# Squared relu on ACT, twelve couples first, finer operand work, and block 2's first half of tokens completed ahead of the second

## The chip, the core and the metric

The kernel runs on one NeuronCore of a Trainium2 chip. The core has five engines with an instruction queue each: PE (TensorE, matrix products into the accumulation memory PSUM), DVE (VectorE), ACT (ScalarE), POOL (GpSimd) and SP (SyncE, which here only issues transfers). They run side by side and wait for each other through semaphores. The metric is device time in microseconds (us), the median of several runs. Before the change it is 2611.3 us (three runs, 2607.07 to 2614.02).

## The reference

The program is two transformer blocks in a row over 1024 tokens of width 1024, all in fp32. Both end in the same kind of MLP. Cut to what matters here:

```python
# block 1: attention over a window of 128 tokens + gated delta rule, then
h = h + jnp.concatenate([attn_out, dn_out], axis=-1) @ w_o
m = rmsnorm(h, norm_mlp)
h = h + jnp.square(jax.nn.relu(m @ w_up)) @ w_down          # w_up 1024x4096, w_down 4096x1024
h = h + sigmoid(rmsnorm(h, norm_ple) @ w_ple_gate) * (p @ w_ple_proj)
x = rmsnorm(h, norm_final)
# block 2: pooled mixer + HGRN2 recurrence in chunks over 6 heads, then
x = x + jnp.concatenate([y_pool, y_hgrn], axis=-1) @ w_out
h2 = rms_norm(x, norm_mlp_g)
x = x + jnp.square(jax.nn.relu(h2 @ w_up)) @ w_down
return rms_norm(x, final_norm_g)
```

## The kernel before

Activations lie transposed, features on the 128 partitions and tokens along the row, in tiles of 128 x 512. So a stream of width 1024 is 8 tiles for each of the two halves of the tokens, h = 0 and h = 1.

**Three products for one.** Each fp32 operand is split into a rounded high part and the rest (`split`, lines 203 and 204: ACT makes the high part by a cast, DVE the rest by a subtraction), and `acc` (lines 223 to 225) sums three matmuls for each pair of 128-blocks. Weights arrive by `load_w` as rows of 1024 (`wr`), and become `wh` and `wl`; there are two buffers for `wr` and three each for `wh` and `wl`.

**The up projection of the MLP** (`mlp`) does without every eighth product: it cuts both factors into 2 x 2 blocks and makes seven products of sums and differences instead of eight. One step n of 16 ("couple") stands for two 128-rows of the hidden layer. Two of its products need only the first half of the tokens: `first` multiplies by b11 and b21, adds both, and gives hidden row 2n of half 0. The others need operands t1, t2, t3, t4 and b22, which are differences between the halves. For the first HP couples `first` runs ahead, before any of the differences is needed; it keeps the product by b11 (tile `r`) in memory (`p1s`). Each hidden tile gets the squared relu in `out` (line 960, one DVE instruction), and SP stores it to `hid`.

**Operands of the MLP** come from `forms`: for a half, `rms` (squares on ACT, line 259, sums on DVE, line 260, a matmul with ones, line 244, the inverse root in small DVE steps, lines 229 to 234), `spread` (lines 270 and 273), the scaling of eight tiles (line 477), and then for half 0 eight splits, for half 1 sixteen differences (line 489) and twenty splits. `forms` is a task that runs beside other work: it stops at each `yield`, and `tick`, called after each product, takes it on by one step. For half 1 it has 15 stops, the first of which is reached when the task is made.

**Ahead of the MLP of block 2** a `weave` of three lanes runs the twelve recurrences (`hgrn`, head j and half h) and lets a second task, `fill`, put its products between their steps, 0.9 of a step for each round. Once the last input projections are made, `fill` is `out_first`: the output projection over six of the eight mixer blocks, 16 tiles of 18 matmuls, stored to `hm`. When all recurrences are over, `out_last` adds the two blocks of the last two heads (6 matmuls a tile, line 408) for half 0, then for half 1, and `forms` is called after each. Block 1 is built the same way.

The lines of Python give the order in which instructions are made; the framework then sets each engine's own order. Each engine works through its order strictly, so what it has to wait for holds up what stands behind.

Of the kernel before, what the change touches and what calls it, by code (L numbers as in the profile page):

```python
# [11 lines left out]
ACTF = mybir.ActivationFunctionType  # L12
ALU = mybir.AluOpType
# [41 lines left out]
FA, POOL_AT = 5, 2  # L55
GATE_HEAD, GATE_TAIL, IN2_HEAD = 4, 4, 6

HP = 10


@with_exitstack
def block_kernel(ctx: ExitStack, tc: tile.TileContext, A):
    nc = tc.nc
    V, SC, G, PE = nc.vector, nc.scalar, nc.gpsimd, nc.tensor
# [247 lines left out]
    def run(*tasks):  # L312
        for t in tasks:
            for _ in t:
                pass
# [70 lines left out]
    def out_first(mix, rows, W, per, src, dst, *halves):  # L386

        n = [0]

        def ev(i, h, ps):  # L390
            n[0] += 1
            f = tt(("sq", "ac")[n[0] % 2])
            nc.sync.dma_start(out=f, in_=src[cs(i), hs(h)])
            V.tensor_tensor(f, ps, f, ALU.add)
            nc.sync.dma_start(out=dst[cs(i), hs(h)], in_=f)

        x = {}
        for h in halves:
            yield from mixed(mix, h, rows)
            x[h] = mix_in(mix, h, rows)  # L400
        yield from proj(x, W, ev, halves, per=per)

    def out_last(mix, rows, W, per, src, h):

        def ev(i, h, ps):
            x = th(h, i)
            nc.sync.dma_start(out=x, in_=src[cs(i), hs(h)])
            V.tensor_tensor(x, ps, x, ALU.add)
            nc.sync.dma_start(out=res[cs(i), hs(h)], in_=x)
            hh[h][i] = x  # L410

        yield from mixed(mix, h, rows)
        yield from proj({h: mix_in(mix, h, rows)}, W, ev, (h,), per=per)
# [46 lines left out]
    def forms(gname, eps):  # L460


        def go(h):
            g = small(gname, 0, KD)
            r = yield from rms(hh[h], eps)

            def pairs(x, new):
                out = []
                for t in x:
                    hi, lo = new(), new()  # L470
                    split(t, hi, lo)
                    out.append((hi, lo))
                return out

            for k in range(KD):
                t = hh[h][k]
                V.scalar_tensor_tensor(t, t, g[:, k:k + 1], r, ALU.mult, ALU.mult)
                if k % 2:
                    yield
            if h == 0:  # L480
                return pairs(hh[0][:4], tu), pairs(hh[0][4:], tu)
            b11, b21, b12, b22 = hh[0][:4], hh[0][4:], hh[1][:4], hh[1][4:]
            out = {}

            for name, x, a, b, new in (("t1", b11, b12, b11, tu), ("t2", b11, b22, b11, tu), ("t3", b12, b22, b12, trr),
                                       ("b22", b22, None, None, trr), ("t4", b21, b11, b21, trr)):
                if a is not None:
                    for i in range(4):
                        V.tensor_tensor(x[i], a[i], b[i], ALU.subtract)
                    yield  # L490
                out[name] = pairs(x, new)
                yield
            return out

        return Parts(go)

    def trr():
        return tr(F32R)

    xs, hm = dram.tile([D, S], F32, name="xs"), dram.tile([D, S], F32, name="hm")  # L500
    res, hid = dram.tile([D, S], F32, name="res"), dram.tile([4 * D, S], F32, name="hid")
    p1s = dram.tile([HP * 128, H], F32, name="p1s")
    hh = [[None] * KD, [None] * KD]


    mix = mix_new("mix1")
# [428 lines left out]
    un = forms("norm_mlp", 1e-6)  # L935
    wa, wb = [[A["w_o"][4 * p + i] for i in range(4)] for p in range(2)]
# [8 lines left out]
    tasks = [lambda lane, n=n: attn_task(lane, n) for n in range(NC)]  # L945
# [7 lines left out]
    def mlp(u, up, dn, between, before=None):  # L953
# [3 lines left out]
        side[0] = 2  # L957

        def out(i, h, c):
            V.scalar_tensor_tensor(c, c, 0.0, c, ALU.max, ALU.mult)  # L960
            nc.sync.dma_start(out=hid[cs(i), hs(h)], in_=c)

        def product(w, i, x):
# [24 lines left out]
        b11, b21 = u[0]  # L988
        for n in range(HP):
            s = tt("r")  # L990
            first(load_w(up[2 * n]), s, tt("f"), n)
            nc.sync.dma_start(out=p1s[cs(n), :], in_=s)
        x = u[1]
        for n in range(16):
# [21 lines left out]
            c = tt("f")  # L1016
# [13 lines left out]
        for h in range(2):  # L1030
            for c4 in range(2):
# [3 lines left out]
                for g in range(8):  # L1035
                    ws = [load_w(dn[4 * g + 2 * c4 + i]) for i in range(2)]
                    x = []
# [9 lines left out]
                for i in range(4):  # L1047
                    m = 4 * c4 + i
                    t = th(h, m)
# [90 lines left out]
    mix = mix_new("mix2")  # L1140
# [156 lines left out]
    t = ins(True, 0, head=IN2_HEAD)  # L1297
# [5 lines left out]
    un = forms("norm_mlp_2", 1e-5)  # L1303
    wa, wb = [A["w_out_2a"][i] for i in range(8)], [A["w_out_2b"][i] for i in range(2)]

    def fills2():
        for j in range(1, 6):
            yield from ins(False, j)
            done.add(j)
        yield from out_first(mix, range(6), wa, 1, xs, hm, 0, 1)  # L1310

    done = {0}

    def task2(lane, j, h):
        while j not in done:
            next(fill, None)
        yield from hgrn(lane, j, h, *i_.pop((j, h)), j >= 4)

    fill = fills2()
    tasks = [lambda lane, j=j, h=h: task2(lane, j, h) for j in range(6) for h in range(2)]  # L1320
    tasks.insert(POOL_AT, lambda lane: pool_mix(lane, *i_.pop("pool")))
    weave(tasks, fill, lambda: R5)

    run(out_last(mix, range(6, 8), wb, 4, hm, 0))
    un()
    run(out_last(mix, range(6, 8), wb, 4, hm, 1))
    un()

# [131 lines left out]
```

## Time and profile before

| | |
|---|---|
| median of three runs | 2611.3 us |
| the profiled execution, its own time | 2615.59 us |
| its span | 2613.2 us, 2.4 us less |
| PE busy | 2503.3 us, 96% of the span |
| weight loads (PEld) | 2010.0 us, 77% |
| DVE, ACT, POOL busy | 1742.7, 987.3, 377.6 us |
| chain that ended last | PE 66%, issue 3%, DVE 3%, POOL 1%, ACT 1% |

The profile's page gives busy time by engine; PE's is modelled, so a busy PE can still run at half its clock. The table of stretches is the better guide: it gives for each stretch how many instructions each engine had in it, and the clock that PE was granted.

### The profile page before, as it was taken

How to read it: one execution, taken by the hardware profiler on the slowest of the kernel's cores; microseconds unless marked ns; L12 is line 12 of the kernel's file. 1: busy time of each engine (PE TensorE's matmuls, PEld its weight loads, DVE VectorE, ACT ScalarE, POOL GpSimd, SP SyncE). 2: the span in 40 equal slices, each digit the busy share in tenths (PEclk: the TensorE clock that was granted, in tenths of full speed). 3: DMA queues.
4: the chain of work that ended last, by engine and by line, in shares of the span. 5: the costliest groups of instructions: out<-in, count | busy, mean ns of one | idle time of the engine just before them, and what ended most of it. 6: DMA issues, size and time to landing. Idle time of an engine off the chain costs nothing.

```text
span 2613.2 us, 41652 instructions
## 1 busy us (share of the span) xinstructions
PE 2503.3 (96%) x16150; PEld 2010.0 (77%) x16150; DVE 1742.7 (67%) x3189; ACT 987.3 (38%) x1632; POOL 377.6 (14%) x430
## 2 busy tenths in 40 slices
PE   6999999998999999999999999999988999999997
PEld 4766777786788888878877878887767888888886
DVE  8787787869887675465457643446599876655653
ACT  4477444324222254344333332333242222444441
POOL 5612222200000000000022343344200000000000
PEclk8999999999999999999999999999989999999998
DMA  5311111354643376446421511113546433765662
GB/s 198 103 55 59 58 49 51 118 197 150 201 156 128 125 258 211 153 158 194 150 79 65 170 58 42 49 45 118 174 172 199 155 127 123 239 200 193 223 196 73
DMA packets 161703, 357.43 MB, mean 137 GB/s; under 512 B 18273, under 2 KB 22753, under 8 KB 161505
## 3 DMA queue, kind: packets, MB, share of 16 engines
q1 hardware_dynamic: 156080, 345.84, 40.2%
q10 hardware_dynamic: 5424, 8.94, 1.0%
q8 instruction: 126, 2.06, 0.3%
q14 instruction: 73, 0.59, 0.1%
HBM read 282.35 MB, written 69.73 MB: 135 GB/s over the span
## 4 chain that ended last, share of the span: by engine, by line
PE 66%; issue 3%; DVE 3%; POOL 1%; ACT 1%; DMA 0%; POOLq 0%; DVEq 0%; ACTq 0%
PE x L225 10%; PE m L223 10%; PE x L224 10%; PE x L223 10%; PE m L225 10%; PE m L224 10%; PE x L1231 1%; POOL u L204 0%; PE x L1240 0%; PE x L1272 0%; PE x L1258 0%; PE x L1274 0%; DVE wl L204 0%; DVE u L204 0%; DMA f<-hid 0%
## 5 line engine op out<-in xcount | busy, mean ns | idle before, releaser
L223 PE MATMUL m<-u,wh 128*128 128x512 f32 x1668 | 673.8, 404 | 11.6 <-ACT wh L203 7.6
L225 PE MATMUL m<-u,wl 128*128 128x512 f32 x1668 | 662.6, 397 | 10.8 <-DVE wl L204 10.6
L224 PE MATMUL m<-u,wh 128*128 128x512 f32 x1668 | 664.5, 399 | 1.9 <-DVE u L204 1.2
L204 DVE TENSOR_TENSOR wl<-wr,wh 128x1024 fp32r<-128x1024 f32 (+2 forms) x265 | 330.1, 1246 | 297.0 <-ACT wh L203 287.0
L203 ACT CAST wh<-wr 128x1024 fp32r<-128x1024 f32 (+2 forms) x265 | 276.0, 1041 | 528.4 <-PE m L224 296.6
L225 PE MATMUL x<-u,wl 128*128 128x512 f32 x1020 | 399.1, 393 | 6.8 <-DVE wl L204 6.8
L223 PE MATMUL x<-u,wh 128*128 128x512 f32 x1020 | 400.2, 393 | 3.3 <-ACT u L203 2.4
L224 PE MATMUL x<-u,wh 128*128 128x512 f32 x1020 | 399.3, 392 | 4.1 <-DVE u L204 4.1
L223 PEld LDWEIGHTS m<-u,wh 128*128 128x128 f32 x1668 | 317.2, 190 | 85.5 <-ACT wh L203 8.8
L225 PEld LDWEIGHTS m<-u,wl 128*128 128x128 f32 x1668 | 317.6, 190 | 80.9 <-DVE wl L204 13.5
L224 PEld LDWEIGHTS m<-u,wh 128*128 128x128 f32 x1668 | 317.4, 190 | 71.7 <-issue 5.6
L225 PEld LDWEIGHTS x<-u,wl 128*128 128x128 f32 x1020 | 193.2, 189 | 48.1 <-DVE wl L204 8.1
L223 PEld LDWEIGHTS x<-u,wh 128*128 128x128 f32 x1020 | 193.5, 190 | 46.7 <-ACT u L203 3.7
L224 PEld LDWEIGHTS x<-u,wh 128*128 128x128 f32 x1020 | 192.7, 189 | 46.0 <-DVE u L204 5.4
L203 ACT CAST u<-f 128x512 fp32r<-128x512 f32 x198 | 122.2, 621 | 188.4 <-PE x L224 76.7
L204 DVE TENSOR_TENSOR u<-f,u 128x512 fp32r<-128x512 f32 x174 | 123.6, 710 | 96.1 <-PE x L224 53.3
L203 ACT CAST wh<-y 128x512 fp32r<-128x512 f32 x91 | 55.1, 621 | 219.8 <-PE x L224 147.1
L204 POOL TENSOR_TENSOR u<-f,u 128x512 fp32r<-128x512 f32 x24 | 35.4, 1475 | 616.3 <-ACT u L203 615.5
L204 DVE TENSOR_TENSOR u<-r,u 128x512 fp32r<-128x512 f32 x128 | 88.0, 688 | 8.5 <-ACT u L203 8.1
L203 ACT CAST u<-r 128x512 fp32r<-128x512 f32 x128 | 79.2, 618 | 14.8 <-DMA r<-hid 12.1
L204 DVE TENSOR_TENSOR wl<-y,wh 128x512 fp32r<-128x512 f32 x91 | 61.8, 682 | 0.0
L260 DVE TENSOR_TENSOR ac<-ac,sq 128x512 f32<-128x512 f32 x70 | 53.8, 768 | 10.9 <-ACT sq L259 8.7
(744 smaller groups left out, 3511.1 us busy)
## 6 DMA issues: line engine op xcount, KB each, us to landing
wr<-in_w_down SPq DMA_DIRECT2D x128, 512.0 KB, 4.0
wr<-in_w_in SPq DMA_DIRECT2D x75, 512.0 KB, 3.4
r<-hid SPq DMA_DIRECT2D x128, 256.0 KB, 4.1
f<-hid SPq DMA_DIRECT2D x128, 256.0 KB, 3.3
y<-in_w_up SPq DMA_DIRECT2D x85, 256.0 KB, 3.2
hid<-f SPq DMA_DIRECT2D x52, 256.0 KB, 2.0
wr<-in_w_up SPq DMA_DIRECT2D x20, 512.0 KB, 4.3
hid<-sq SPq DMA_DIRECT2D x32, 256.0 KB, 3.1
```

Source lines behind the costliest of these rows:

```text
L203: SC.copy(hi, src)
L204: eng.tensor_tensor(lo, src, hi.bitcast(F32), ALU.subtract)
L223: PE.matmul(ps, whi[:, s], xh, start=(first and k == 0), stop=False)
L224: PE.matmul(ps, whi[:, s], xl, start=False, stop=False)
L225: PE.matmul(ps, wlo[:, s], xh, start=False, stop=(last and k == len(x) - 1))
L260: V.tensor_tensor(a, a, sq, ALU.add)
L1231: PE.matmul(ps[p, c * 16:c * 16 + 16], k[:, m], odd(q[:, m], l), start=True, stop=True)
```

## The change

It has four parts. The squared relu becomes two ACT instructions (Relu, then Square, in place) instead of one of DVE. HP goes from 10 to 12. `forms` stops after every two differences and every two splits of half 1, which makes 24 stops out of 15; half 0 has no new stops. In block 2, `fill` makes the output projection for half 0 alone, then that for half 1 as far as the last two heads of half 0 still lack, then completes half 0 with `out_last` and starts its `forms`, and only then goes on with half 1; `w_out`'s first part is so loaded and split once for each half. The order of the last four recurrences becomes head 4 and head 5 of half 0, then both of half 1.

```diff
-HP = 10
+HP = 12
...
             def pairs(x, new):
                 out = []
-                for t in x:
+                for i, t in enumerate(x):
                     hi, lo = new(), new()
                     split(t, hi, lo)
                     out.append((hi, lo))
+                    if i % 2 and h:
+                        yield
                 return out
...
             if h == 0:
-                return pairs(hh[0][:4], tu), pairs(hh[0][4:], tu)
+                b11 = yield from pairs(hh[0][:4], tu)
+                return b11, (yield from pairs(hh[0][4:], tu))
...
                 if a is not None:
                     for i in range(4):
                         V.tensor_tensor(x[i], a[i], b[i], ALU.subtract)
-                    yield
-                out[name] = pairs(x, new)
-                yield
+                        if i % 2:
+                            yield
+                out[name] = yield from pairs(x, new)
...
         def out(i, h, c):
-            V.scalar_tensor_tensor(c, c, 0.0, c, ALU.max, ALU.mult)
+            SC.activation(c, c, ACTF.Relu)
+            SC.activation(c, c, ACTF.Square)
             nc.sync.dma_start(out=hid[cs(i), hs(h)], in_=c)
...
-        yield from out_first(mix, range(6), wa, 1, xs, hm, 0, 1)
+        yield from out_first(mix, range(6), wa, 1, xs, hm, 0)
+        rest = out_first(mix, range(6), wa, 1, xs, hm, 1)
+        while not all((0, i) in mix["done"] for i in (6, 7)) and next(rest, "end") != "end":
+            yield
+        yield from out_last(mix, range(6, 8), wb, 4, hm, 0)
+        un()
+        yield from rest
...
-    tasks = [lambda lane, j=j, h=h: task2(lane, j, h) for j in range(6) for h in range(2)]
+    tasks = [lambda lane, j=j, h=h: task2(lane, j, h) for j, h in
+             [(j, h) for j in range(4) for h in range(2)] + [(4, 0), (5, 0), (4, 1), (5, 1)]]
...
-    run(out_last(mix, range(6, 8), wb, 4, hm, 0))
-    un()
     run(out_last(mix, range(6, 8), wb, 4, hm, 1))
     un()
```

The order on the engines moves at three places. The first is DVE in block 1's MLP, where the first couples run beside the operands of half 1. `wl` is the rest of a couple's weights, L984 (L988 after) the sum that ends a couple, L489 (L492) the differences, and L204 into `u` or into a, b, c, d, e, g the rests of the operands. Before, from the end of the fifth couple to that of the sixth:

```order
L984 TENSOR_TENSOR f<-x_7227,r 128x512
L204 TENSOR_TENSOR u<-y_6619,u 128x512
L960 SCALAR_TENSOR_TENSOR f<-f 128x512
L489 TENSOR_TENSOR y_6813<-y_6931,y_6813 128x512
L489 TENSOR_TENSOR z<-y_6948,z 128x512
L204 TENSOR_TENSOR wl<-wr,wh 128x1024
L204 TENSOR_TENSOR a_7271<-y_6751,a_7270 128x512
L204 TENSOR_TENSOR b_7275<-y_6792,b_7274 128x512
L204 TENSOR_TENSOR c_7279<-y_6813,b_7278 128x512
...
L204 TENSOR_TENSOR g_7315<-y_6948,g_7314 128x512
L984 TENSOR_TENSOR f<-m,r 128x512
```

and now, between the same two sums:

```order
L988 TENSOR_TENSOR f<-x_7211,r 128x512
L204 TENSOR_TENSOR u<-x,u 128x512
L492 TENSOR_TENSOR y_6751<-z,y_6751 128x512
L492 TENSOR_TENSOR y_6792<-z,y_6792 128x512
L204 TENSOR_TENSOR wl<-wr,wh 128x1024
L204 TENSOR_TENSOR u<-y_6619,u 128x512
L492 TENSOR_TENSOR y_6813<-y_6931,y_6813 128x512
L492 TENSOR_TENSOR z<-y_6948,z 128x512
L988 TENSOR_TENSOR f<-m,r 128x512
```

Where fourteen instructions stood from one sum to the next there are now eight, the squared relu is gone from DVE, and `wl` is that of the eighth couple where it was that of the sixth.

The second place is ACT in the same stretch, after the change: L963 and L964 are Relu and Square, L985 copies the product by b11, `wh` is the high part of the weights of a later couple.

```order
L203 CAST b_7376<-y_6792 128x512
L203 CAST wh<-wr 128x1024
L203 CAST b_7403<-y_6813 128x512
L963 ACTIVATE f<-f 128x512
L203 CAST c_7407<-z 128x512
L964 ACTIVATE f<-f 128x512
L985 COPY r<-m 128x512
L203 CAST wh<-wr 128x1024
L963 ACTIVATE f<-f 128x512
L964 ACTIVATE f<-f 128x512
L985 COPY r<-x_7339 128x512
```

Each Relu stands ahead of casts that have nothing to do with it, and has to wait for DVE's sum of its couple.

The third place is PE near the end of the weave of block 2. L1235 and L1244 (L1231 and L1240 before) are levels of the last recurrence (head 5, half 1), L1256 (L1252) turns its keys, L433 turns a finished head, and the rows by `u` are matmuls of the output projection. Before:

```order
L1231 MATMUL x_18045<-g_16475,tmp_16477 32x16 x16
...
L1240 MATMUL x_18105<-g_16475,tmp_16477 32x32 x8
...
L1240 MATMUL x_18142<-g_16475,tmp_16477 64x64 x4
...
L1252 MATMUL x_18174<-consts_90,tmp_16477 128x128 x4
```

and now:

```order
L1235 MATMUL x_18162<-g_16545,tmp_16547 32x16 x16
L225 MATMUL m<-u,wl 128x512
L433 MATMUL x_18095<-consts_90,y_18030 128x128 x4
L1244 MATMUL x_18198<-g_16545,tmp_16547 32x32 x8
...
L1244 MATMUL x_18223<-g_16545,tmp_16547 64x64 x4
L225 MATMUL m<-u,wl 128x512
L1256 MATMUL x_18243<-consts_90,tmp_16547 128x128 x4
```

Before, 13, 18 and 18 matmuls of the output projection stood in the three gaps left out; now it is 1 (beside the L433), 5 and 1. Behind the last recurrence, 36 of them stand ahead of the sum over half 0 (L244), 2 more ahead of the last head's L433, and then 100 ahead of the MLP's first full product; before, 39 stood ahead of that L433, 26 from there to the sum over half 0, and 27 more ahead of its spread (L273), behind which the MLP began.

## Rows read from the trace of the kernel before

**Rows 1.** Stretches at both junctions: us, PE, PEld, DVE, ACT, POOL busy (x instructions), PEclk, DMA.
```profile
600.00:625.00 25.00, 22.48 (x93) 17.67 (x92) 22.23 (x43) 10.88 (x18) 0.00 (x0) 0.86 0.35 125
625.00:650.00 25.00, 23.64 (x103) 18.84 (x101) 23.06 (x37) 13.43 (x22) 0.00 (x0) 1.00 0.50 168
650.00:675.00 25.00, 17.29 (x60) 12.70 (x59) 22.40 (x34) 6.98 (x11) 0.00 (x0) 0.86 0.65 197
1900.00:1925.00 25.00, 18.37 (x69) 12.55 (x68) 20.31 (x40) 8.93 (x14) 2.02 (x1) 0.84 0.64 221
1925.00:1950.00 25.00, 23.08 (x96) 17.61 (x97) 24.50 (x48) 12.18 (x20) 0.00 (x0) 0.89 0.42 137
1950.00:1975.00 25.00, 18.61 (x71) 14.83 (x70) 24.35 (x39) 11.96 (x20) 0.00 (x0) 0.86 0.37 127
1975.00:2000.00 25.00, 23.93 (x104) 19.19 (x104) 22.71 (x35) 8.23 (x13) 0.00 (x0) 1.00 0.84 275
2000.00:2025.00 25.00, 25.00 (x112) 20.68 (x112) 21.61 (x36) 5.82 (x10) 0.00 (x0) 1.00 0.49 160
```

**Rows 2.** PE in order of time, block 1: start, us, instruction [idle before, releaser].
```profile
601.15 0.39 PE L224 MATMUL m<-u,wh 128*128 128x512 f32 x1
601.38 0.39 PE L225 MATMUL m<-u,wl 128*128 128x512 f32 x1
...
616.50 0.66 PE L244 MATMUL x<-ac,ones 128*32 128x128 f32 x8 [2.04 <-DVE ac L260]
...
639.14 0.50 PE L225 MATMUL m<-u,wl 128*128 128x512 f32 x1 [1.36 <-DVE wl L204]
...
654.25 0.79 PE L225 MATMUL x<-u,wl 128*128 128x512 f32 x1 [3.93 <-DVE wl L204]
...
671.32 0.80 PE L225 MATMUL x<-u,wl 128*128 128x512 f32 x1 [1.79 <-DVE wl L204]
```

**Rows 3.** PE in order of time, block 2's junction.
```profile
1902.08 0.66 PE L433 MATMUL x<-consts,y 128*128 128x128 f32 x4 [2.03 <-POOL y L429]
...
1906.50 0.63 PE L223 MATMUL m<-u,wh 128*128 128x512 f32 x1
1906.93 0.63 PE L224 MATMUL m<-u,wh 128*128 128x512 f32 x1
...
1926.92 0.80 PE L224 MATMUL x<-u,wh 128*128 128x512 f32 x1 [4.07 <-DVE u L204]
...
1965.95 0.79 PE L225 MATMUL m<-u,wl 128*128 128x512 f32 x1 [6.39 <-DVE wl L204]
...
1981.12 0.50 PE L225 MATMUL x<-u,wl 128*128 128x512 f32 x1 [1.07 <-DVE wl L204]
```

**Rows 4.** DVE in order of time, block 1, around its longest wait.
```profile
652.38 0.68 DVE L489 TENSOR_TENSOR z<-y,z 128x512 f32<-128x512 f32 x1
652.98 1.22 DVE L204 TENSOR_TENSOR wl<-wr,wh 128x1024 fp32r<-128x1024 f32 x1
654.11 0.68 DVE L204 TENSOR_TENSOR a<-y,a 128x512 fp32r<-128x512 f32 x1
```

**Rows 5.** Groups of instructions: DVE's scaling, ACT's squares and casts.
```profile
L477 DVE SCALAR_TENSOR_TENSOR y<-y,smalls,x 128x512 f32<-128x512 f32 x18 | 12.7, 740 | 0.2 <-PE x L273 0.2
...
L259 ACT ACTIVATE sq<-y 128x512 f32<-128x512 f32 x35 | 21.9, 628 | 21.8 <-DVE y L1051 8.4 <-DVE ac L260 7.1 <-DVE y L408 5.4
...
L203 ACT CAST wh<-y 128x512 fp32r<-128x512 f32 x91 | 55.1, 621 | 219.8 <-PE x L224 147.1 <-PE m L224 67.9 <-DVE y L1002 4.8
```

**Rows 6.** PE, DVE and POOL in order of time: two levels of a recurrence, and a head's end.
```profile
1867.80 0.45 PE L1231 MATMUL x<-g,tmp 128*32 128x16 f32 x32
...
1869.53 0.45 PE L1231 MATMUL x<-g,tmp 128*32 128x16 f32 x32
...
1890.80 0.39 PE L1274 MATMUL x<-y,g 128*128 128x128 f32 x2
...
1899.53 2.49 POOL L429 TENSOR_TENSOR y<-y,hr 128x512 f32<-128x512 f32 x1 [19.79 <-DVE hr L234]
```

## The prediction, made before the changed kernel ran

> **What bounds the kernel now.** I read the table of stretches first. Over most of the two MLPs PE runs without a hole: from 2000 to 2025 us it has 112 instructions in 25 us and the full clock of 2.4 GHz [rows 1]. Two neighbouring full matmuls start 0.23 us apart there (0.227 over longer runs) [rows 2]. So what DVE or ACT save inside the MLPs buys nothing by itself; only holes in PE's work can be won back. The reader should look for the stretches with fewer than 112. There are two of a size, both where an MLP takes over from the mixer ahead of it. I call 600 to 675 us junction A (block 1) and 1900 to 2000 us junction B (block 2).
>
> The counts give their price. A has 93 + 103 + 60 = 256 instructions where three full stretches have 336; 10 of them are small (the sums and the spread), worth about 1.5 us in all, as eight of them take 0.66 us [rows 1, 2]. So 90 matmuls are missing: 90 x 0.227 - 1.5 = 18.9 us lost. B has 340 where 448 would stand, 24 of them small and worth some 3.5 us: 132 x 0.227 - 3.5 = 26.5 us lost [rows 1]. Together 45 us, the most that this change could give.
>
> Then PE's own rows show the reasons. In A it waits 2.04 us for DVE's sums of squares of the second half, and then 1.36, 3.93 and 1.79 us for `wl`, the rest of a couple's weights, which DVE makes [rows 2]. In B it waits 2.03 us for POOL's scaling of the last head, 4.07 us for the rests of the first half's operands, and 6.39 and 1.07 us for `wl` [rows 3]. Nearly all of it is DVE, which is busy 22 to 24.5 us of each 25 there [rows 1]. The waits add up to less than the loss. The remainder is the clock: behind a wait of 2 us PE starts two matmuls 0.43 us apart, the 1.2 GHz level, and the stretches around it were granted 0.84 to 0.89 on average [rows 1, 3].
>
> **Part 1: twelve couples, smaller portions, relu off DVE (both junctions).** A couple is 24 matmuls, 24 x 0.227 = 5.45 us of PE. DVE starts an instruction on 128 x 512 every 0.60 us and needs 1.13 us for `wl` on 128 x 1024 [rows 4]. A couple costs it `wl`, the sum and the squared relu, 2.33 us before and 1.73 after. The operands of the second half are 8 scalings (740 ns each, 0.66 where they overlap), 16 differences and 20 rests: 5.3 + 9.6 + 12 = 26.9 us [rows 4, 5]. Before, their 14 remaining stops last seven couples, 38.2 us of PE, for which DVE has 26.9 + 7 x 2.33 = 43.2 us of work and the inverse root's small steps on top. It cannot keep up, and its order makes it worse: `wl` of the sixth couple stands behind differences, and eight operand rests stand ahead of the next sum. After, 23 stops last 11.5 couples, 62.7 us of PE, against 26.9 + 11.5 x 1.73 = 46.8 us. In the order of DVE after the change I find eight instructions from sum to sum, one or two of them `wl`: 7 x 0.60 + 1.13 = 5.3 us, just inside 5.45. `wl` moves two couples further ahead. So the waits for `wl` in A and their half clock go. Of A's 18.9 us the first wait, with the slow matmuls behind it, stays, because nothing ahead of it moved in DVE's order: 2.0 us of waiting and 16 matmuls at 0.43 instead of 0.227, 3.3 us, some 5.3 in all. I add 1 us for a margin of only 0.15 us per couple. A ends at 6.3 instead of 18.9: **-12.6 us**, with bounds of -8 (two waits like that of 1.79 with their slow matmuls remain) and -14. In B the waits of 6.39 and 1.07 us and the slow matmuls behind the first (12 x 0.2 = 2.4) are of this kind; of these 9.9 us I leave 1: **-8.9 us**.
>
> The two more couples cost nothing on PE: their products are only made earlier. They store and load `p1s` twice more, by DMA, which is busy 0.35 to 0.84 of the time at the junctions [rows 1].
>
> ACT takes over 128 hidden tiles. Its Square on such a tile takes 628 ns [rows 5]; Relu on the same tile is not in the trace, and I take the same. That is 128 x 2 x 0.63 = 161 us more for ACT, for 128 x 0.60 = 77 us less on DVE. ACT is busy 5.8 of 25 us in the full MLP stretch [rows 1], so PE's work covers this. The Trainium skill ("ScalarE: Activation LUTs", section "Rules for kernel authors") says to use VectorE for relu and multiplication, not ScalarE. The rows agree that ACT is the dearer engine here, two times 0.63 us against 0.60; they also show that ACT has the time, which decides as long as it does not hold others up (the third rival).
>
> **Part 2: the first half of tokens completed ahead (junction B).** What goes: the sums, the root and the scaling of half 0 no longer stand between the last output projection and the MLP. That is the rest of B's loss, 26.5 - 9.9 = 16.6 us. What comes in its place, step by step along PE's order after the change:
> - The last recurrence loses its cover. Two levels with five matmuls between them start 1.73 us apart [rows 6], and PE did not idle between them, so a level needs at most 1.73. Now the last levels have 1 to 5 matmuls between them, 0.2 to 1.1 us. By my count of the gaps that is about 2 us of waiting. Bounds: 0, and 5 if DVE, which has the sums of half 0 in between, delays its steps.
> - The last head's end. From its last matmul to the end of POOL's scaling took 1890.80 to 1902.02, 11.2 us [rows 6], with additions of rms between the root's small steps. These are there again: six additions, two `wl` and three adds of output tiles. PE now has 38 matmuls, the sum and little else for that time: 38 x 0.227 + 0.7 = 9.3 us. I expect 11 to 13 us of latency, so a wait of 2 to 4 us, at the sum over half 0 and at L433, and the slow clock behind it: 4.6 + 2.6 = 7.2 us. Before, the same place cost 2.03 us and its slow matmuls, so this is no gain.
> - Then 100 matmuls, 22.7 us, cover DVE's root, 8 scalings, 8 rests, 16 sums of output tiles and four `wl`. 8 x 0.66 + 24 x 0.60 + 4 x 1.13 = 24.2 us, of which the last rests are needed one product later: 1 us of waiting.
> - The sums of half 1 are then late as they are in A: 2 us and some slow matmuls, 4 us. Bounds 2 and 5.3.
> Sum 2 + 7.2 + 1 + 4 = 14.2 us in place of 16.6: **-2.4 us**, with bounds of +4 and -11 (where neither the head's end nor the sums of half 1 stop PE). The second loading of `w_out`'s first part is eight rows of 768, for DVE about 0.9 us each and for ACT less; they lie in a part where PE is fed by 18 matmuls at a time, 4.1 us, and cost nothing unless DVE falls behind, when it is the 5 us above.
>
> **The sum.** -12.6 - 8.9 - 2.4 = -23.9 us. The profiled execution took 2615.6 us (span 2613.2 and 2.4 around it) and comes to 2591.7. The median of the runs shown, 2611.3, is 4.3 us below that execution, so I forecast 2611.3 - 23.9 = **2587.4 us**. With all bounds on the good side, -14 - 9.9 - 11 = -35, it is 2576; on the bad side, -8 - 6 + 4 = -10, it is 2601.
>
> **The rivals.**
> 1. *Only the couples gain; junction B swaps one wait for another.* The last recurrence and the last head end late, DVE is full (24.5 of 25 us in B [rows 1]), and its second half comes no earlier than before. Then A's 12.6 remain: 2599. For it: the head's end already waits on an in-order DVE; against it: the wait of 6.39 us has nothing to do with the head. 17%.
> 2. *It does not do what it says.* DVE needs 5.3 us of the 5.45 in each couple. If each hand-over between ACT and DVE costs 0.5 us, it falls behind as before, the holes only spread over twelve couples, and nothing is won: 2611. For it: the small margin; against it: over the twelve couples DVE has 15 us to spare. 8%.
> 3. *ACT's queue: slower.* Each Relu stands ahead of casts that do not need it, and waits for a sum by DVE, which waits for PE. The casts of the MLP's weights already start late: 147.1 + 67.9 us of ACT's idle time ahead of the `wh` casts ended when PE gave back a buffer [rows 5]. If of 0.60 us for DVE's sum and 1.2 for Relu and Square just 0.4 us reach PE for each of 128 tiles, that is +51 us: 2638. It decides from 24 / 128 = 0.19 us a tile, where all the gain is used up. Against it: three `wh` buffers hold two products each of 12 matmuls, 5.45 us of work, so a cast 1.8 us late is still in time. The Trainium skill ("TensorE: Matmul & The Clock Gate", section "Architectural detail") says that ACT and DVE take instructions strictly in turn; that ACT casts stop behind one that waits is what this rival needs. 9%.
>
> **How the numbers follow.** The forecast has 66%, with its own range of 2576 to 2601. This kernel's measurement can't tell less than 0.3%, some 8 us, from no change. The forecast lies beyond that on the fast side, bar the very end of its range. Rival 1 lies mostly there too (13 of its 17 points; 4 within). Rival 2 is no change. Of rival 3, 7 points are slower and 2 within. So faster 0.66 + 0.13 = 0.79, same 0.04 + 0.08 + 0.02 = 0.14, slower 0.07. For the range I take the forecast's bounds on the good side, 2575, and on the bad side most of rival 1 with the price of a worse tail: 2605. Above that lie rivals 2 and 3, 15%.
>
> **What would show it.** In the profile after: at A, 93 in the first stretch as before and close to 112 in the two behind it; no wait of PE for `wl` over 1 us. At B, the wait of 6.39 us gone, but still a wait at the last head's L433 and at the sum over the second half. In the MLP stretches 112 in 25 us with DVE down by about 3 us and ACT up by some 7. It would be wrong if PE waits for ACT's casts inside the MLPs, or if the recurrences end later by more than the 5 us allowed.

## The result and the profile after

The changed kernel takes 2585.95 us (median of 4 runs, 2584.28 to 2588.66) where the kernel before, measured beside it, takes 2612.2 (2607.07 to 2614.02). The ratio is 0.9897, with a 95% interval of 0.9884 to 0.9909. That is 26.2 us less, against 23.9 forecast. The profiled execution has a span of 2582.2 us.

The stretches come first, as [rows 1] did for before. The work lies earlier by now, so junction A is again 600 to 675 us, but junction B is 1850 to 1975 (its last four stretches are shown).

```profile
600.00:625.00 25.00, 22.25 (x103) 17.55 (x102) 22.08 (x44) 11.34 (x19) 0.00 (x0) 1.00 0.35 130
625.00:650.00 25.00, 24.66 (x109) 20.11 (x108) 25.00 (x37) 19.41 (x33) 0.00 (x0) 1.00 0.62 211
650.00:675.00 25.00, 25.00 (x112) 20.68 (x111) 24.24 (x37) 16.70 (x27) 0.00 (x0) 1.00 0.85 286
...
1875.00:1900.00 25.00, 24.23 (x111) 18.34 (x110) 22.64 (x46) 9.14 (x14) 1.04 (x1) 1.00 0.73 246
1900.00:1925.00 25.00, 21.88 (x98) 16.46 (x97) 21.94 (x42) 13.18 (x21) 0.00 (x0) 1.00 0.71 240
1925.00:1950.00 25.00, 25.00 (x112) 20.70 (x111) 24.78 (x38) 18.90 (x33) 0.00 (x0) 1.00 0.56 189
1950.00:1975.00 25.00, 25.00 (x112) 20.70 (x111) 23.23 (x36) 16.19 (x26) 0.00 (x0) 1.00 0.91 302
...
2000.00:2025.00 25.00, 25.00 (x112) 20.72 (x111) 17.37 (x28) 11.57 (x20) 0.00 (x0) 1.00 0.49 165
```

The 256 instructions of A have become 324. By the prediction's own count that is (336 - 324 + 10) x 0.227 - 1.5 = 3.5 us lost instead of 18.9. DVE is at least as full as before (22 to 25 us of each 25), but PE's holes have become small, and the granted clock is 1.00 in each stretch of both junctions, where five of seven had 0.84 to 0.89 [rows 1]. In the MLP (last row, against the last of [rows 1]) PE still has 112, DVE 4.2 us less and ACT 5.8 us more.

PE's rows in block 1, to set against [rows 2]:

```profile
616.86 0.43 PE L244 MATMUL x<-ac,ones 128*32 128x128 f32 x8 [2.04 <-DVE ac L260]
618.00 0.50 PE L225 MATMUL m<-u,wl 128*128 128x512 f32 x1 [0.71 <-DVE wl L204]
...
634.48 0.50 PE L225 MATMUL m<-u,wl 128*128 128x512 f32 x1 [0.34 <-DVE wl L204]
```

The first wait is the same to a hundredth. The three for `wl` of [rows 2] (1.36, 3.93 and 1.79) are gone, and so are two waits of before that [rows 2] leaves out, the second of them for ACT:

```profile
662.53 0.50 PE L225 MATMUL m<-u,wl 128*128 128x512 f32 x1 [1.05 <-DVE wl L204]
...
668.34 0.50 PE L223 MATMUL x<-u,wh 128*128 128x512 f32 x1 [0.94 <-ACT wh L203]
```

What is left is 0.71, where before had 0.48, and 0.34. PE's rows in block 2, to set against [rows 3], from the last recurrence on:

```profile
1848.01 0.50 PE L224 MATMUL m<-u,wh 128*128 128x512 f32 x1 [0.57 <-DVE u L204]
...
1854.17 0.45 PE L1235 MATMUL x<-g,tmp 128*32 128x16 f32 x32 [0.55 <-DVE hr L234]
...
1856.19 0.66 PE L433 MATMUL x<-consts,y 128*128 128x128 f32 x4 [1.15 <-POOL y L429]
...
1860.34 0.66 PE L1256 MATMUL x<-consts,tmp 128*128 128x128 f32 x4 [0.69 <-POOL tmp L1252]
...
1867.26 0.50 PE L223 MATMUL m<-u,wh 128*128 128x512 f32 x1 [0.64 <-DVE y L408]
...
1869.74 0.50 PE L223 MATMUL m<-u,wh 128*128 128x512 f32 x1 [0.82 <-DVE y L408]
...
1877.02 0.42 PE L244 MATMUL x<-ac,ones 128*32 128x128 f32 x8 [0.20 <-DVE ac L260]
...
1878.50 0.66 PE L433 MATMUL x<-consts,y 128*128 128x128 f32 x4 [0.39 <-POOL y L429]
...
1904.51 0.50 PE L223 MATMUL m<-u,wh 128*128 128x512 f32 x1 [0.77 <-DVE z L408]
...
1909.28 0.50 PE L225 MATMUL x<-u,wl 128*128 128x512 f32 x1 [1.53 <-DVE wl L204]
...
1921.86 1.10 PE L273 MATMUL x<-ac,ones 128*128 128x512 f32 x2 [0.81 <-DVE ac L270]
```

The four waits of [rows 3], 1 to 6.4 us, and one of 1.49 us for ACT that [rows 3] leaves out (at 1922.36 us) have turned into many short ones, the longest 1.53. Over the whole program the groups of PE's operand waits say the same. Before (columns: group | busy, mean ns | idle before and its releasers):

```profile
L223 PE MATMUL m<-u,wh 128*128 128x512 f32 x1668 | 673.8, 404 | 11.6 <-ACT wh L203 7.6 <-ACT tmp L574 1.6 <-ACT u L203 1.5
...
L225 PE MATMUL m<-u,wl 128*128 128x512 f32 x1668 | 662.6, 397 | 10.8 <-DVE wl L204 10.6
...
L225 PE MATMUL x<-u,wl 128*128 128x512 f32 x1020 | 399.1, 393 | 6.8 <-DVE wl L204 6.8
```

and after:

```profile
L223 PE MATMUL m<-u,wh 128*128 128x512 f32 x1676 | 673.4, 402 | 14.3 <-ACT wh L203 7.4 <-ACT u L203 2.4 <-ACT tmp L577 1.7
...
L225 PE MATMUL m<-u,wl 128*128 128x512 f32 x1676 | 662.5, 395 | 2.5 <-DVE wl L204 2.4
L225 PE MATMUL x<-u,wl 128*128 128x512 f32 x1012 | 393.8, 390 | 1.5 <-DVE wl L204 1.5
```

Waiting for `wl` fell from 17.4 to 3.9 us. Waiting for ACT's `wh` casts, in the first group, was 7.6 and is 7.4, although ACT now does 256 instructions more.

To place the gain, I numbered the full matmuls (L223 to L225) in order of their start, 9312 in each trace, and compared the start of the same number in two traces. From number 1440 to 1800 lies A, from 5800 to 6800 B. The changed kernel's 1440th starts 0.4 us later than before's, its 1800th 15.2 earlier, its 5800th 16.2, its 6800th 31.2 and its last 31.0. So A gained 15.6 us, B 15.0, and everything else together 0.4. These are two single executions: that of before lies 3.4 us above its median and that of after 1.7 below, which is why they add up to 31 and not 26.

The same starts show what the gain is made of. Between two of these numbers PE either waits, or starts full matmuls, or does the small ones. In A the waits fell from 11.6 to 3.1 us, and what full matmuls took beyond one per 0.227 us fell from 7.8 to 1.0; in B from 21.2 to 12.6 and from 17.4 to 11.3. The small ones changed by 0.2 to 0.3 us.

### The profile page after: what moved, and what is told of

It is laid out like the page before. It is cut to its first block, busy times and chain, and to the rows that moved or that the text cites. A ratio compares the mean times of both kernels' runs of the same rounds, so it can differ in the third digit from the quotient of the medians.

```text
span 2582.2 us, 41944 instructions
## 1 busy us (share of the span) xinstructions
PE 2489.7 (96%) x16150; PEld 2000.7 (77%) x16150; DVE 1677.1 (65%) x3065; ACT 1142.7 (44%) x1892; POOL 377.3 (15%) x430
## 4 chain that ended last, share of the span: by engine, by line
PE 79%; DVE 9%; issue 5%; POOL 3%; DMA 3%; ACT 1%; SPq 0%; DVEq 0%; ACTq 0%; POOLq 0%
PE m L223 13%; PE m L224 13%; PE m L225 13%; PE x L225 11%; PE x L223 11%; PE x L224 11%; DVE wl L204 1%; POOL u L204 1%; PE x L1235 1%; PE x L673 1%; DVE ac L260 1%; PE x L711 1%; DVE u L204 1%; DVE y L745 0%; PE x L702 0%
## 5 line engine op out<-in xcount | busy, mean ns | idle before, releaser
L223 PE MATMUL m<-u,wh 128*128 128x512 f32 x1676 | 673.4, 402 | 14.3 <-ACT wh L203 7.4
L225 PE MATMUL m<-u,wl 128*128 128x512 f32 x1676 | 662.5, 395 | 2.5 <-DVE wl L204 2.4
L204 DVE TENSOR_TENSOR wl<-wr,wh 128x1024 fp32r<-128x1024 f32 (+2 forms) x277 | 343.1, 1239 | 296.1 <-ACT wh L203 284.6
L203 ACT CAST wh<-wr 128x1024 fp32r<-128x1024 f32 (+2 forms) x277 | 286.8, 1035 | 519.5 <-PE m L224 305.0
L223 PE MATMUL x<-u,wh 128*128 128x512 f32 x1012 | 395.2, 391 | 0.4 <-ACT u L203 0.4
L225 PE MATMUL x<-u,wl 128*128 128x512 f32 x1012 | 393.8, 390 | 1.5 <-DVE wl L204 1.5
L224 PE MATMUL x<-u,wh 128*128 128x512 f32 x1012 | 393.8, 389 | 0.0
L223 PEld LDWEIGHTS m<-u,wh 128*128 128x128 f32 x1676 | 316.4, 189 | 89.8 <-ACT wh L203 8.3
L225 PEld LDWEIGHTS m<-u,wl 128*128 128x128 f32 x1676 | 316.9, 189 | 71.1 <-DVE wl L204 4.3
L223 PEld LDWEIGHTS x<-u,wh 128*128 128x128 f32 x1012 | 190.4, 188 | 41.4 <-ACT u L203 1.3
L225 PEld LDWEIGHTS x<-u,wl 128*128 128x128 f32 x1012 | 190.0, 188 | 41.4 <-DVE wl L204 2.0
L224 PEld LDWEIGHTS x<-u,wh 128*128 128x128 f32 x1012 | 190.0, 188 | 40.5 <-issue 0.7
L204 DVE TENSOR_TENSOR u<-f,u 128x512 fp32r<-128x512 f32 x174 | 123.1, 708 | 107.5 <-PE x L224 49.9
L204 POOL TENSOR_TENSOR u<-f,u 128x512 fp32r<-128x512 f32 x24 | 35.5, 1478 | 600.3 <-ACT u L203 599.5
L204 DVE TENSOR_TENSOR u<-r,u 128x512 fp32r<-128x512 f32 x128 | 88.1, 689 | 4.7 <-ACT u L203 4.5
L963 ACT ACTIVATE f<-f 128x512 f32<-128x512 f32 x56 | 35.4, 632 | 108.8 <-DVE f L1021 99.0
L260 DVE TENSOR_TENSOR ac<-ac,sq 128x512 f32<-128x512 f32 x70 | 53.9, 770 | 11.3 <-ACT sq L259 8.7
```

The lines of the kernel that those rows point to most:

```text
L203: SC.copy(hi, src)
L204: eng.tensor_tensor(lo, src, hi.bitcast(F32), ALU.subtract)
L223: PE.matmul(ps, whi[:, s], xh, start=(first and k == 0), stop=False)
L224: PE.matmul(ps, whi[:, s], xl, start=False, stop=False)
L225: PE.matmul(ps, wlo[:, s], xh, start=False, stop=(last and k == len(x) - 1))
L260: V.tensor_tensor(a, a, sq, ALU.add)
```

## The experiments

The table has each run's median, its ratio to the kernel before with the 95% interval, and by how much its A and B are shorter than before's (positions as above). Stretches whose code is the same in two kernels differ by up to 6 us between two profiles (number 1440 starts 6.1 us later in one of the runs below than in before; e4's A, with the code of before, came out 2.3 us shorter). I take differences in A or B under 2.5 us as nothing.

| run | us | ratio | A | B |
|---|---|---|---|---|
| the change | 2585.95 | 0.9897 [0.9884, 0.9909] | 15.6 | 15.0 |
| e11, the change again | 2585.91 | 0.9902 [0.9888, 0.9917] | 14.8 | 16.1 |
| e1, relu on DVE | 2588.74 | 0.9906 [0.9892, 0.9919] | 13.3 | 13.6 |
| e2, order back | 2591.18 | 0.9917 [0.9903, 0.9930] | 14.6 | 10.9 |
| e8, ten couples, small portions | 2588.92 | 0.9905 [0.9890, 0.9919] | 16.0 | 13.3 |
| e5, twelve, large portions | 2602.10 | 0.9959 [0.9947, 0.9972] | 6.9 | 6.2 |
| e3, ten, large portions | 2602.38 | 0.9956 [0.9942, 0.9970] | 9.0 | 5.5 |
| e4, order alone | 2610.30 | 0.9989 [0.9980, 0.9998] | 2.3 | 3.5 |
| e6, task order back | 2592.29 | 0.9914 [0.9898, 0.9931] | 14.6 | 13.6 |
| e9, half 0's rests on POOL | 2587.22 | 0.9894 [0.9878, 0.9911] | 15.8 | 12.3 |
| e10, more fill in the tail | 2592.80 | 0.9926 [0.9913, 0.9938] | 14.6 | 8.3 |

**Undo one part each.** e1 undoes the move of the squared relu, e2 block 2's order (all its hunks; that of the tasks is e6's edit, below), e3 the couples and portions.

```diff
 e1
-            SC.activation(c, c, ACTF.Relu)
-            SC.activation(c, c, ACTF.Square)
+            V.scalar_tensor_tensor(c, c, 0.0, c, ALU.max, ALU.mult)
 e2
-        yield from out_first(mix, range(6), wa, 1, xs, hm, 0)
-        rest = out_first(mix, range(6), wa, 1, xs, hm, 1)
...
+        yield from out_first(mix, range(6), wa, 1, xs, hm, 0, 1)
...
+    run(out_last(mix, range(6, 8), wb, 4, hm, 0))
+    un()
 e3
-HP = 12
+HP = 10
-                for i, t in enumerate(x):
+                for t in x:
...
-                    if i % 2 and h:
-                        yield
...
-                        if i % 2:
-                            yield
-                out[name] = yield from pairs(x, new)
+                    yield
+                out[name] = pairs(x, new)
+                yield
```

> The changed kernel with the squared relu back on DVE as one instruction; all else as changed. My theory (DVE's work against PE's over the couples decides): DVE has 26.9 + 11.5 x 2.33 = 53.7 us of work for the 62.7 us of the couples, so it still keeps up on average; each junction loses 0 to 2 us, 2586 to 2590 us. Rival (the relu is what makes each couple fit: 5.3 + 0.6 = 5.9 us of DVE for 5.45 of PE): 0.45 us a couple, some 5 us at each junction, 2596 us, with waits of PE for the rests of the weights. Both: the full MLP stretches stay at 112 instructions in 25 us.

> The changed kernel with block 2's order of before (order of the recurrences, output projection for both halves together, both completions behind the weave); relu, twelve couples and portions as changed. My theory (the order was worth 2.4 us, since new waits take the place of the old): 2588 us, junction A unchanged, at junction B the waits at the last head and ahead of the MLP's first product (2.0 and 4.1 us before) are back, but nothing else. Rival (the order carries what junction B gained beyond the 8.9 us that I gave to the couples, 15.7 - 8.9 = 6.8): 2593 us. Rival 2 (it carries nearly all of B): 2600 us.

> The changed kernel with ten couples and the coarse portions of before (15 stops); relu on ACT and block 2's order as changed. My theory: seven couples give 38.2 us for 26.9 + 7 x 1.73 = 39.0 us of DVE work and the root's small steps, so DVE still falls behind, by about half as much as before: 5 to 8 us back at each junction, 2597 to 2602 us, with waits of PE for the rests of the weights of 2 us and more. Rival (with the relu gone from DVE neither the couples nor the portions matter): 2586 to 2589 us.

e1 costs 2.8 us, and the intervals overlap: with small portions DVE can nearly afford the relu. e2 costs 5.2 us, 4.1 of them in B; at 2591.18 it lies between its theory's 2588 and the first rival's 2593. e3 costs 16.4, more than the other two together; at its median of 2602.38 it lies just above what its theory gave. In e2 the waits of the old order are back:

```profile
1892.35 0.66 PE L433 MATMUL x<-consts,y 128*128 128x128 f32 x4 [2.04 <-POOL y L429]
...
1895.30 0.80 PE L223 MATMUL m<-u,wh 128*128 128x512 f32 x1 [0.78 <-DVE y L408]
...
1912.59 0.51 PE L223 MATMUL x<-u,wh 128*128 128x512 f32 x1 [1.49 <-ACT u L203]
...
1917.15 0.80 PE L224 MATMUL x<-u,wh 128*128 128x512 f32 x1 [4.05 <-DVE u L204]
```

The 2.04 and 4.05 are the 2.03 and 4.07 of [rows 3]; the 6.39 and 1.07 for `wl` are not there. So the couples' part and the order's part are separate in B, as the prediction had them. The two full matmuls that take 0.80 instead of 0.50 us in these rows stand at the lower clock: the stretches 1894 to 1899 and 1914.5 to 1919.5 us were granted 0.50.

**One part alone, and the couples apart from the portions.** e4 keeps the order alone (e3's edit and e1's together). e5 keeps HP = 12 with the large portions, e8 takes HP = 10 with the small ones:

```diff
 e5
-                for i, t in enumerate(x):
+                for t in x:
...
-                out[name] = yield from pairs(x, new)
+                out[name] = pairs(x, new)
+                yield
 e8
-HP = 12
+HP = 10
```

> The kernel before with only block 2's order changed; relu on DVE, ten couples, coarse portions. My theory: 2.4 us less than before, 2609 to 2610 us, junction A as before; the wait of 6.4 us for the rests of a couple's weights stays at B. Rival (order carries 6.8 us or more of B by itself): 2605 us or less. Third case (the order pays only where the couples no longer wait, since what it wins ahead of the MLP is lost again in the couples): no change, 2612 us.

> The changed kernel with the coarse portions of before (15 stops), but twelve couples. The 15 stops still end after seven couples, so by my theory (DVE's work against PE's while the stops last) two more couples behind them change nothing: 2600 to 2603 us, as with ten couples and coarse portions (2602.4), with the same holes at both junctions. Rival (the number of couples is what gives DVE time): 2586 to 2590 us.

> The changed kernel with ten couples, fine portions kept. The first 20 of 23 stops lie beside ten couples, 54.5 us of PE for 26.9 + 10 x 1.73 = 44.2 us of DVE work, the last three come at once behind them. By my theory that is enough: 2586 to 2589 us, perhaps 1 us lost at each junction behind the tenth couple. Rival (twelve couples are needed): 2592 us or more, with waits of PE at the start of the steps that need the differences.

e4 is 2.7 us faster than before, about as its theory had it, and its B still has a wait of 6.79 us for `wl`: the order does not cure that. e5 is e3 to within 0.3 us, and e8 is the change to within 3.0. So of the first part it is the portions that act; the two more couples give between nothing and 3 us, which these runs can't separate. PE's rows of e5 in A, after the first two waits, show what twelve couples leave:

```profile
651.64 0.71 PE L225 MATMUL x<-u,wl 128*128 128x512 f32 x1 [1.94 <-DVE wl L204]
...
660.07 0.50 PE L225 MATMUL m<-u,wl 128*128 128x512 f32 x1 [0.98 <-DVE wl L204]
...
666.81 0.50 PE L225 MATMUL x<-u,wl 128*128 128x512 f32 x1 [0.63 <-DVE wl L204]
```

The first of these `wl` is made at 650.38, at the end of a string on DVE that has no hole from 642.55 on; the second stands behind eight rests and a sum that had to wait itself:

```profile
642.55 0.69 DVE L985 TENSOR_TENSOR f<-x,r 128x512 f32<-128x512 f32 x1 [0.57 <-ACT u L203]
...
650.38 1.22 DVE L204 TENSOR_TENSOR wl<-wr,wh 128x1024 fp32r<-128x1024 f32 x1
...
658.19 0.69 DVE L985 TENSOR_TENSOR f<-m,r 128x512 f32<-128x512 f32 x1 [1.78 <-ACT wh L203]
658.80 1.22 DVE L204 TENSOR_TENSOR wl<-wr,wh 128x1024 fp32r<-128x1024 f32 x1
```

In the same stretch of e8 PE is full, with the ten couples of before:

```profile
650.00:675.00 25.00, 25.00 (x112) 20.69 (x111) 23.71 (x37) 17.99 (x31) 0.00 (x0) 1.00 0.80 272
```

The small portions do two things at once. They cut the blocks that stand ahead of a `wl`, and, being 24 stops and not 15, they spread the same 26.9 us of operand work over more couples: by the prediction's numbers 2.3 us beside each couple instead of 3.8. A full DVE alone is not the fault, since the change's DVE has no hole at all from 625 to 650 us and PE hardly waits; but no run keeps the 15 stops and cuts the blocks, so which of the two counts is not shown.

Relu and portions overlap in what they win. From e4, moving the relu alone (e3) gives 7.9 us; portions and couples alone (e1) give 21.6; both together (the change) 24.4.

**Can what is left be had?** e6 keeps half 0 completed ahead but puts the recurrences back into their old order. e9 has POOL make every second rest of half 0, so that DVE comes to half 1's sums of squares sooner. e10 gives the last recurrence 1.8 steps of other work per round in place of the usual rate. e11 is the change again, on the same chip as these.

```diff
 e6
-    tasks = [lambda lane, j=j, h=h: task2(lane, j, h) for j, h in
-             [(j, h) for j in range(4) for h in range(2)] + [(4, 0), (5, 0), (4, 1), (5, 1)]]
+    tasks = [lambda lane, j=j, h=h: task2(lane, j, h) for j in range(6) for h in range(2)]
 e9
-                    split(t, hi, lo)
+                    split(t, hi, lo, G if i % 2 and h == 0 else V)
 e10
+        tail[0] = True
         yield from out_last(mix, range(6, 8), wb, 4, hm, 0)
+        tail[0] = False
...
-    weave(tasks, fill, lambda: R5)
+    weave(tasks, fill, lambda: 1.8 if tail[0] else R5)
```

> The changed kernel with the recurrences in their old order (head 4 both halves, then head 5 both halves), the fill as changed. Head 5 of half 0 then ends later, fewer tiles are left behind it, and more tiles of half 1 go ahead. My theory: junction B loses part of what the order gave (4 us between the changed kernel and the one with the order back), 2587 to 2590 us. Rival (the order of the recurrences is what makes it work; with it back the first half is complete too late): 2592 us or more.

> The changed kernel with every second rest of half 0's operands (4 of 8 in each MLP) on POOL, which has nothing to do there. The wait of 2.2 us for the sums of half 1 at junction A, and the one for the rests of the weights at B, lie behind these rests on DVE. If DVE's queue is what holds them (my theory), 4 x 0.60 = 2.4 us of DVE go and the wait at A falls to under 0.5 us: 1 to 2 us at each junction, 2582 to 2584 us. Rival (POOL is slow, 1.04 to 2.5 us on such a tile, so the operands come later and PE waits for them): same or up to 4 us slower.

> The changed kernel, but while the fill completes half 0 (tiles of 6 matmuls) it gives 1.8 tiles a round of the recurrences in place of 0.9, so that the last levels of the last recurrence have 6 matmuls and more between them instead of 1 to 5. In the changed kernel PE lost some 5 us in that tail (waits of 0.5 to 1.4 us at the levels, the turned keys and the last but one head). If the cover is what they lack (my theory), the tail wins 2 to 4 us, some of which is given back because fewer matmuls are left behind the recurrence: 2583 to 2585 us. Rival (the waits only move to the last head's turn, whose end depends on DVE's queue): same as the changed kernel within 1 us.

> The changed kernel once more, unaltered, on the same chip as the kernel with the higher rate. Expected 2584 to 2589 us. In its profile the first wait at junction A (2.2 us, for the sums of half 1) should be there again; whether PE's clock falls behind it is open: if it falls by the length of the wait alone, it stays at 2.4 GHz as in the first profile; if it is chance, either may come.

None beats the change. e6's median falls where its rival had it (2592 or more) and is 6.4 us above e11, but its B gains only 2.5 us less than e11's and 1.4 less than the change's; the rest lies in stretches that the edit doesn't touch. What the task order alone is worth stays open between 0 and some 3 us. e9 was to take 2582 to 2584 us and takes what the change takes. In it the waits of 2.04 and 0.71 us were not won but spread over three places, 2.70 us together:

```profile
618.29 0.47 PE L223 MATMUL m<-u,wh 128*128 128x512 f32 x1 [1.18 <-DVE y L408]
...
624.55 0.43 PE L244 MATMUL x<-ac,ones 128*32 128x128 f32 x8 [0.76 <-DVE ac L260]
...
630.72 1.12 PE L273 MATMUL x<-ac,ones 128*128 128x512 f32 x2 [0.76 <-DVE ac L270]
```

What moved to POOL came back on DVE, whose own rests became longer while POOL made its share:

```profile
613.14 1.63 POOL L204 TENSOR_TENSOR u<-y,u 128x512 fp32r<-128x512 f32 x1 [3.55 <-ACT u L203]
615.23 3.45 POOL L204 TENSOR_TENSOR u<-y,u 128x512 fp32r<-128x512 f32 x2 [0.46 <-ACT u L203]
...
613.52 2.33 DVE L204 TENSOR_TENSOR wl<-wr,wh 128x1024 fp32r<-128x1024 f32 x1
615.77 1.78 DVE L204 TENSOR_TENSOR u<-z,u 128x512 fp32r<-128x512 f32 x1
```

In the change the same two take 1.22 and 0.68 us. With 1.15 instead of 0.68 for the next one that is 2.7 us more on DVE, against the 2.4 that were to go.

e10 fell the other way: it was to be 1 to 3 us faster than the change and is 6.9 slower than e11. The short waits at the last levels became shorter (0.32 for 0.55 at L1235; the 0.69 at L1256 is gone) and that at L433 longer (1.30 for 1.15), but the matmuls that moved ahead of the end of the recurrence are missing behind it: 14 full ones stand there ahead of the sum over half 0, where the change has 36. Three views of e10 show the new wait, PE's, DVE's and SP's own queue (in SP's the columns are line <- what it waited for: us in total, times, longest):

```profile
1874.79 0.39 PE L1278 MATMUL x<-y,g 128*128 128x128 f32 x2
1880.58 0.79 PE L223 MATMUL m<-u,wh 128*128 128x512 f32 x1 [5.40 <-DVE x L408]
```

```profile
1879.83 0.69 DVE L408 TENSOR_TENSOR x<-m,x 128x512 f32<-128x512 f32 x1 [4.81 <-DMA x<-hm]
```

```profile
SPq L407 <- PE x L1278: 3.6, 1, 3.6
```

`out_last` loads the partial sums `hm` back into a tile that the recurrence's last matmuls (L1278) still use. SP waits for them, the load lands 4.3 us after its issue, and PE, which has nothing left but the product that needs this sum, stands for 5.40 us and goes on at the lower clock. In the change the same load is issued at 1866.46 and holds DVE's sum for 0.17 us only:

```profile
1869.86 0.69 DVE L408 TENSOR_TENSOR x<-m,x 128x512 f32<-128x512 f32 x1 [0.17 <-DMA x<-hm]
```

There PE still has other matmuls to do. (The wait of 2.2 us and the 5 us of waits that the expectations of e9 and e10 name are 2.04 and 4.0 by the rows.)

## Why the prediction was right, and where it was not

**What bounds it: right.** Only A and B moved (15.6 and 15.0 of 31.0 us between the profiles), and the MLPs, with 161 us more work on ACT, stayed where they were: from number 1800 to 5800 the shift changes by 1.0 us.

**A, forecast -12.6, bounds -8 to -14; measured -14.6 to -16.0 in the six runs with small portions, relu on ACT and half 0's rests on DVE,** so beyond the better bound. (As e4's A came out 2.3 shorter with unchanged code, that much of it may belong to the one profile of before.) The mechanism is as it was put: no wait for `wl` over 0.71 us, the first wait unchanged at 2.04. The term that was mis-sized is what stays, 5.3 + 1 us. It took 16 slow matmuls, 3.3 us, behind the first wait as given; before's trace has 13 there, 2.8 us, and the profile after none: the 22 instructions of 620 to 625 us were granted 1.00, and what stays is 3.5 us by count. The statement that the first stretch would show 93 again failed for the same reason: it shows 103. That was luck in part (last section): in e11, with slow matmuls there, 2.75 us of waits and 2.1 of slow clock stay, near the 5.3. The reason for the gain was also told too widely: HP = 12 was counted as a part of it (62.7 us of PE over 11.5 couples), and e5 and e8 show that the portions do most or all of it. Whether by the order in DVE's queue or by the work beside each couple is open; e3, e5 and e8 came out within 0.4 us of the ranges that were reckoned from the work beside the couples.

**B, couples, forecast -8.9; measured -10.9 (e2).** Right: the waits of 6.39 and 1.07 and their slow matmuls are gone, and nothing of the 1 us left for them shows.

**B, order, forecast -2.4, bounds +4 to -11; measured -3.5 (e4 against before) and -4.1 (the change against e2).** Right in sign; its terms came out thus. (The bound of -11 is mis-added: without the 7.2 and the 4 us, 3 stay of 14.2, and 16.6 less 3 is 13.6.)
- The tail, 2 us: the waits from 1830 to 1861 us add up to 3.98 us (the first four rows shown, one of 0.70 and one of 0.32), and 1.95 stood there before, at two heads' L433 (0.78 and 1.17). So 2.0, as said.
- The head's end, 7.2 us: mis-sized. The latency was right: from the last L1278 at 1866.23 to L433 at 1878.50 it is 12.3 us, for which 11 to 13 stood. But the waits in it are four of 0.20 to 0.82, 2.05 in all, and none leads to the lower clock. The prediction took a wait of 2 to 4 us and the slow clock behind it, 7.2 in all. POOL's scaling also took 1.04 us here where it took 2.49 [rows 6] (and takes 2.49 again in e2, with the old order). The row of the change:

```profile
1877.41 1.04 POOL L429 TENSOR_TENSOR y<-y,hr 128x512 f32<-128x512 f32 x1 [16.60 <-DVE hr L234]
```

- The 100 matmuls, 1 us: 0.77 and 1.53, so 2.3. The 24.2 us of DVE's work for 22.7 us of PE's was short, and the last `wl` paid.
- The sums of half 1, 4 us: 0.81 at L273 and 0.17 at an earlier one, so about 1.

These sum to 7.4 us, not 14.2. The measured gain is nonetheless only 4 us, not 16.6 - 7.4 = 9. Counted over all of B, from e2 to the change, PE's waits fall from 13.7 to 12.6 us only, what full matmuls take beyond 0.227 us each from 14.0 to 11.3, and the small ones by 0.3. So the order traded waits for almost as many others, as the prediction had it, and most of its gain in these two profiles is clock (granted 0.98 over B in e2, 1.00 in the change). That part is not safe: e1, e6, e8 and e9 have the new order as well (e6 all but the tasks), and there the matmuls' term is 12.7 to 14.5. The medians (e2 5.2 us, e4 2.7) say that the order gains something; how much of it is the clock's chance stays open.

**Rival 1 (only the couples gain; B swaps one wait for another) is refuted** as to B, which gains 15.0 us, 10.9 of them without the new order. Of the order alone it is nearer the truth: there waits do take each other's place. **Rival 2 (it does not do what it says) is refuted** by the 112 in 650 to 675 us. **Rival 3 (ACT's queue) is refuted twice:** the waits for `wh` stayed where they were over the program, and e1, which takes Relu and Square off ACT again, is not faster. (With large portions it shows in small: e3 waits 1.78 and 0.40 us for `wh` at A.) Relu took what was assumed for it:

```profile
L963 ACT ACTIVATE f<-f 128x512 f32<-128x512 f32 x56 | 35.4, 632 | 108.8 <-DVE f L1021 99.0 <-DVE f L988 9.8
L964 ACT ACTIVATE f<-f 128x512 f32<-128x512 f32 x56 | 35.4, 632 | 1.6
```

ACT does wait for DVE's sums, 108.8 us ahead of these 56, as that rival said; the casts behind were still in time. The Trainium skill ("ScalarE: Activation LUTs", section "Rules for kernel authors") would have kept the relu on VectorE. By cost per tile the rows agree, 2 x 0.632 us against one pitch of 0.60; by the time of the kernel e1 does not: the cheaper engine was the one that was short, and putting the relu back on it wins nothing and loses up to 2.8 us.

**The sum** came within 2.3 us of the measured 26.2, and that is closer than its terms: A and the couples of B were under-estimated by 2 to 3 and by 2 us, the order by 1 to 2. Between the two profiles the gain is 31 us; it is 26 between the medians because these two executions lie 3.4 us above and 1.7 below them. That this made up for most of the terms' errors is luck.

## What to carry to other kernels

Where a short engine feeds a full one, look at how its side work is dealt out before taking work off it: dealing it in twos, over more steps, won more here (21.6 us with the couples, against 7.9) than taking the relu, a quarter of the engine's own work per couple, off it. Two cures for one shortage do not add up, so time each alone and both together before either is given its price. When work is moved ahead of a chain to cover it, ask what then covers the chain's end, and which loads wait for a tile that the chain still holds.

## What the runs showed of the hardware that was not expected

The same waits at A, 2.04 us at L244 and 0.48 to 0.71 us for `wl` behind it, stand in eleven of the twelve profiles (not in e9's). In nine of them the granted clock falls behind these waits, in the change's and e8's it does not. The stretch 620 to 625 us of the change (columns as in [rows 1]; the clock is the third number from the end):

```profile
620.00:625.00 5.00, 5.00 (x22) 3.79 (x21) 2.63 (x11) 1.98 (x3) 0.00 (x0) 1.00 0.60 218
```

and of e11, the same kernel in another execution:

```profile
620.00:625.00 5.00, 5.00 (x18) 3.92 (x17) 3.35 (x14) 1.47 (x2) 0.00 (x0) 0.74 0.69 215
```

With PE busy all of 620 to 625 us there are 22 and 18 instructions: four matmuls, 0.9 us, by nothing that the kernel does differently. So a slow stretch that a profile shows behind a wait of 2 us is a price with a chance, not a fixed one, and two profiles can differ by a few us for it. The Trainium skill ("TensorE: Matmul & The Clock Gate", section "Part 1: The HAM clock gate (the "warmup" mystery)") says that the number of slow matmuls at a kernel's start varies from run to run of one kernel; these rows show the like behind a wait in the middle of one.

The other thing is POOL and DVE side by side. The scaling of the last head takes POOL 1.04 us in the change and e10 but 2.49 before and in e2, where eleven of the twelve heads take 1.04. In before and e2 DVE makes a `wl` meanwhile, in the change and e10 it does not; in e9 it is DVE that takes longer, 2.33 us for a `wl`. In the change the 219 `wl` of this size that run without a POOL instruction of over 0.5 us beside them take 1.18 to 1.43 us, the other 40 up to 2.3. So the two hold each other up at times; which pairs of instructions do so was not tried.
